# Conv taps, gates, late weights and branch A's projection put in another order in a gated conformer decoder step

## Chip, cores and metric

The kernel runs on one core of a Trainium2 chip. The metric is the device time of one execution in microseconds. The kernel before takes 1085.22 us, the median of 3 runs (1084.03 to 1085.56).

## The reference

One layer of a decoder trunk on 1024 prompt positions plus 16 meta tokens and on 8 x 8 sample positions, all in fp32, with D = 1024 channels:

```python
h = rmsnorm(x, norm_g)
z = jnp.einsum('btd,de->bte', h, w_in)
a_val, a_gate, a_silu, p_in, p_silu, g_a, g_b = jnp.split(z, idx, axis=-1)
u = a_val * jax.nn.sigmoid(a_gate)
c, new_conv = causal_depthwise_conv(u, buf_conv, conv_w, conv_b)   # width 31
c = jax.nn.silu(layernorm(c, ln_g, ln_b)) * jax.nn.silu(a_silu)
br_a = jnp.einsum('btc,cd->btd', c, w_conv_out)
pooled, new_pool = multiscale_pool(p_in, buf_pool, start_pos)      # 4 groups: mean over 2/4/8/16 - token
q = jnp.einsum('btgc,gce->btge', pg, w_pool_mix).reshape(B_, T_, D_POOL)
q = q * pool_scale * jax.nn.silu(p_silu)
br_b = jnp.einsum('btc,cd->btd', q, w_pool_out)
merged = jax.nn.sigmoid(g_a) * br_a + jax.nn.sigmoid(g_b) * br_b
return x + jnp.einsum('btd,de->bte', merged, w_out), new_conv, new_pool
```

A final RMSNorm follows, and the last 30 conv inputs and 15 pool inputs are returned as states.

## The kernel before

Channels lie on the 128 partitions, in 8 blocks of 128; the 1088 positions lie along the free axis, in two halves of 544 (552 with the meta tokens in front). Every fp32 product is made of three products of rounded parts, high x high, high x low and low x high (`gemm`, L149). A *split* makes the parts of an operand: `split` casts the high part on ScalarE and subtracts it on VectorE (L119, L120); `split_dma` casts on ScalarE, negates the high part on ScalarE and lets GpSimd issue a transfer that accumulates the raw operand onto it (L124 to L126).

The stages, with their times in the profiled execution:

1. 0 to 81 us: six of the eight pool input blocks (`pp`) while x and weights arrive, and the RMS norm of x.
2. 88 to 164 us: `Block` products in the order g0 v0 p6 p7 g1 v1 (a conv gate, its value, two pool blocks, and so on), 96 matmuls each (`pg`, `pv`, `pp`).
3. 164 to 683 us: 22 pairs of column blocks in the order g1 v1 g2 v2 g3 v3, q0 to q3 (pool SiLU gate), b0 to b3 (merge gate b), a0 to a3 (merge gate a), s0 to s3 (conv SiLU gate). `seven` makes each pair by a Strassen-type scheme: seven products of 24 matmuls into three PSUM tiles x, v and y. y starts as a copy of x, made by ScalarE (`py`, L467); parts of x are kept in `c2` and `c4`, and VectorE subtracts v from them (L480 for `c4`, which has to read v before the product `d` is added to v, and L489 for `c2`). `put` then evacuates each result with ScalarE (sigmoid or silu, L583). In the q and b pairs the pool mix (`Mix`) puts four products of 12 matmuls (`pmix`) between, whose results a `gate` on VectorE (L832) multiplies with silu of the gate.
4. 683 to 791 us: branch B's projection, `ppo`, 8 output blocks by 2 halves, 48 matmuls each. VectorE multiplies each result with the merge gate `lb` (L997), which SP loads from DRAM.
5. 791 to 830 us: LayerNorm over channels of the conv result: `lcsum` sums the eight blocks, `pt_mean` multiplies it with ones on TensorE, `centre` subtracts the mean (L965), squares on ScalarE (L967) and sums (L969), `suml_var` and `pt_var` give the variance, `root` its inverse root.
6. 830 to 884 us: `branch_a(i)` for each channel block i: times the inverse root (L979), silu on ScalarE (L980), times the gate `lsa` by halves (L982) and a split into the operand `cx`.
7. 882 to 976 us: branch A's projection, `pco`, 8 output blocks d by 2 halves, 48 matmuls each; VectorE multiplies it with `lga` and adds `ltb` (L1068, L1069), and a split gives the operand `mx`. Its first group begins as the `cx` appear.
8. 976 to 1082 us: the product with w_out (`pwo`), the residual and the final norm.

The depthwise conv is VectorE work without a fixed place: per channel block one tap by L661, 30 taps by L663 and four sample groups (L673 to L678). These are pieces in a list, `todo`, with costs. `fill(until)` takes pieces from it while VectorE's modelled time `clock["dve"]` is below `until`; the caller passes TensorE's modelled time, `clock["pe"]`, which `step` advances by 3.0 us for each product. So the written order of VectorE's instructions is set where `fill` is called. Each engine works through its own instructions in the written order (a manual schedule); `defer(n, f)` runs f n steps later. PSUM has four tiles of two banks (`bank2`), weights and halves have pools of fixed size.

## Time and profile before

| | before |
|---|---|
| median of 3 runs | 1085.22 us (1084.03 to 1085.56) |
| the profiled execution | 1084.14 us, its span 1082.4 us |
| TensorE matmul busy | 963.5 us, 89% of the span |
| VectorE busy | 795.6 us, 74% |
| ScalarE busy | 456.1 us, 42% |
| GpSimd busy | 158.7 us, 15% |
| chain that ended last | TensorE 65%, VectorE 14%, ScalarE 9%, DMA 5%, issue 4% |
| granted TensorE clock, mean | 0.94 |

The table is to be read with the stages above: the shares are means over stages in which different engines set the pace. In 500 to 678 us TensorE is busy 175.06 of 178 us; in 818 to 882 us 16.39 of 64 us, at a granted clock of 0.50, which is 1.2 GHz where 1.00 is 2.4 GHz. [...]

### The profile page before, as it was taken

The numbers are of one execution on the slowest core, as the hardware profiler recorded it, in microseconds if no ns is written. First come the engines' busy times: TensorE is split into PE (matmuls) and PEld (weight loads), VectorE is DVE, ScalarE is ACT, GpSimd is POOL, SyncE is SP. The second block draws the span as 40 slices with busy tenths as digits, with TensorE's granted clock in tenths as the row PEclk, the third lists the DMA queues.
The fourth block names the chain that finished last, engine by engine and source line by source line (L and its number), as shares of the span: only waits on it lengthen the run. The fifth ranks groups of instructions, "written<-read, shape, count | busy, mean of one in ns | idle before, by whom it ended". The sixth has DMA issues, their size and how long they took to land.

```text
span 1082.4 us, 17920 instructions
## 1 busy us (share of the span) xinstructions
PE 963.5 (89%) x7032; PEld 932.5 (86%) x7032; DVE 795.6 (74%) x1043; ACT 456.1 (42%) x761; POOL 158.7 (15%) x192
## 2 busy tenths in 40 slices
PE   9997998999999899999999999979921359999996
PEld 8997998999999889999999999979921259998885
DVE  6466869997887698898999998389975554455343
ACT  7634245544554445456555656200035332134111
POOL 0001422322231121232322322000000000000000
PEclk9998999999999899999999999989965559999998
DMA  8333796788695766979889899733430344433222
GB/s 294 114 95 113 215 248 144 162 217 218 146 222 118 202 185 181 256 179 227 190 214 220 200 226 260 262 126 132 167 135 21 83 122 133 132 108 136 98 78 97
DMA packets 100900, 180.67 MB, mean 167 GB/s; under 512 B 21456, under 2 KB 24912, under 8 KB 100816
## 3 DMA queue, kind: packets, MB, share of 16 engines
q1 hardware_dynamic: 70720, 121.98, 35.0%
q0 software_dynamic: 20880, 39.66, 21.2%
q10 hardware_dynamic: 9216, 17.90, 4.4%
q8 instruction: 55, 0.90, 0.3%
q14 instruction: 29, 0.24, 0.1%
HBM read 93.92 MB, written 48.71 MB: 132 GB/s over the span
## 4 chain that ended last, share of the span: by engine, by line
PE 65%; DVE 14%; ACT 9%; DMA 5%; issue 4%; SPq 1%; ACTq 1%; DVEq 0%
PE pco L149 9%; PE ppo L149 7%; PE pp L149 6%; PE px_s L149 5%; PE px_a L149 5%; PE px_q L149 4%; PE pwo L1108 4%; PE px_v L149 3%; PE px_b L149 3%; PE px_g L149 3%; PE pg L149 3%; DVE c L663 2%; PE pv_v L149 2%; DMA xr<-in_xres 2%; PE pv_g L149 1%
## 5 line engine op out<-in xcount | busy, mean ns | idle before, releaser
L663 DVE SCALAR_TENSOR_TENSOR c<-ce,pv,c 128x1024 f32<-128x1024 f32 x240 | 308.1, 1284 | 5.2
L149 PE MATMUL pco<-cx,w_co 128*128 128x272 f32 x768 | 108.4, 303 | 47.5 <-ACT cx L119 47.5
L149 PEld LDWEIGHTS pco<-cx,w_co 128*128 128x128 f32 x768 | 103.9, 200 | 52.1 <-ACT cx L119 50.1
L149 PE MATMUL ppo<-q,w_po 128*128 128x272 f32 x768 | 98.6, 291 | 8.0 <-DVE w_po L120 7.1
L149 PEld LDWEIGHTS ppo<-q,w_po 128*128 128x128 f32 x768 | 97.9, 191 | 8.7 <-DVE w_po L120 7.5
L1108 PE MATMUL pwo<-wo,mx 128*128 128x512 f32 x336 | 79.4, 394 | 0.0
L1108 PEld LDWEIGHTS pwo<-wo,mx 128*128 128x128 f32 x336 | 63.1, 188 | 14.8
L149 PE MATMUL pp<-xg,wh_p 128*128 128x276 f32 x384 | 65.4, 291 | 0.8 <-ACT xg L217 0.5
L149 PEld LDWEIGHTS pp<-xg,wh_p 128*128 128x128 f32 x384 | 54.8, 188 | 1.8 <-ACT xg L217 0.9
L119 ACT CAST mx<-lga 128x544 fp32r<-128x544 f32 x16 | 10.4, 648 | 71.4 <-DVE lga L1069 71.4
L1127 DVE TENSOR_TENSOR xr<-pwo,xr 128x1024 f32<-128x1024 f32 (+1 forms) x9 | 9.9, 1105 | 41.5 <-PE pwo L1108 25.8
L149 PE MATMUL pp<-xg,wl_p 128*128 128x276 f32 x192 | 40.0, 289 | 0.0
L119 ACT CAST w_po<-raw_po 128x512 fp32r<-128x512 f32 x16 | 9.5, 619 | 67.7 <-DMA raw_po<-in_w_po 57.3
L1068 DVE TENSOR_TENSOR lga<-pco,lga 128x544 f32<-128x544 f32 x16 | 11.6, 724 | 33.7 <-PE pco L149 33.7
L1090 ACT ACTIVATE sq<-xr 128x1024 f32<-128x1024 f32 (+1 forms) x9 | 8.7, 965 | 65.5 <-DVE xr L1127 65.5
L149 PE MATMUL px_q<-tT,woq_q 128*128 128x272 f32 x192 | 29.7, 318 | 6.6 <-ACT py_q L467 6.6
L149 PEld LDWEIGHTS px_q<-tT,woq_q 128*128 128x128 f32 x192 | 28.5, 217 | 7.2 <-ACT py_q L467 7.2
L149 PE MATMUL pg<-hx,w_g 128*128 128x276 f32 x192 | 27.3, 306 | 7.0 <-ACT w_g L119 7.0
L149 PEld LDWEIGHTS pg<-hx,w_g 128*128 128x128 f32 x192 | 26.6, 203 | 7.6 <-ACT w_g L119 7.3
L149 PEld LDWEIGHTS pp<-xg,wl_p 128*128 128x128 f32 x192 | 30.2, 188 | 0.0
L149 PE MATMUL px_b<-tT,woq_b 128*128 128x272 f32 x192 | 25.6, 289 | 3.0 <-ACT py_b L467 3.0
L149 PEld LDWEIGHTS px_b<-tT,woq_b 128*128 128x128 f32 x192 | 24.5, 188 | 3.7 <-ACT py_b L467 3.7
(403 smaller groups left out, 2201.3 us busy)
## 6 DMA issues: line engine op xcount, KB each, us to landing
lraw<-d_raw SPq DMA_DIRECT2D x16, 276.0 KB, 3.4
d_pool<-pool SPq DMA_DIRECT2D x8, 544.0 KB, 4.5
lp<-d_pool SPq DMA_DIRECT2D x16, 272.0 KB, 4.8
lq<-d_q SPq DMA_DIRECT2D x16, 272.0 KB, 5.3
lb<-d_sgb SPq DMA_DIRECT2D x16, 272.0 KB, 4.5
d_tb<-lb SPq DMA_DIRECT2D x16, 272.0 KB, 2.1
lsa<-d_sa SPq DMA_DIRECT2D x16, 272.0 KB, 5.2
ltb<-d_tb SPq DMA_DIRECT2D x16, 272.0 KB, 2.8
```

Source lines behind the costliest of these rows:

```text
L119: act.copy(dst_h, src)
L149: pe.matmul(out[:, u, : hi - lo], w(k, a), xs(k, b)[:, lo:hi], start=first and k == ks[0] and i == 0, stop=last and k == ks[-1] and i == 2 ...
L663: dve.scalar_tensor_tensor(c, s, wk, c, ALU.mult, ALU.add)
L1068: dve.tensor_tensor(of_half(ga), ps, of_half(ga), ALU.mult)
L1090: act.activation(sq[:rows, c], xr[:, c], AF.Square, accum_out=a1 if ns[0] else a0)
L1108: pe.matmul(ps[:, n - ns[0]], x(k), wo[k][n][w], start=(k == 0 and s == 0), stop=(k == NK - 1 and s == len(passes) - 1),)
L1127: dve.tensor_tensor(v3(xr[:, c], 512), ps[:, : len(ns)], v3(xr[:, c], 512), ALU.add)
```

## The change

- `LAG`: `fill` goes on until VectorE's modelled time is 1.5 us past the time it is given. In `seven`, in `Mix.gate`, in the glu and in the `ppo` loop `fill` is now called ahead of the evacuation instead of behind it.
- In `seven`, one more `yield` lets the caller issue the copy `py` of a pair one part earlier.
- The first tap of each conv block is made by ScalarE (`begin`), at the first sample group of the block before it.
- The weights of g0 are loaded and split ahead of the norm's products; those of v0 are loaded there.
- In the `ppo` loop the weights of `ppo` 1 to 7 and `w_co0`, `w_co1` are split by `split_dma`, `lb` is loaded one block ahead, and the loads of the conv blocks are spread over two blocks.
- In `branch_a`, `cx` of blocks 1, 3 and 5 is split by `split_dma`.
- The first two output blocks of `pco` are accumulated in four PSUM tiles together, channel block by channel block; `w_co2` is split only afterwards.

```diff
-T_PRODUCT = 3.0
+
+T_PRODUCT, LAG = 3.0, 1.5
...
     plain1(1)
+    ops[0].load()
+    ops[0].split(split)
+    ops[1].load()
     keep_raw(1, 1, outs[1])
     plain1(2)
...
     def fill(until=None):
-        while todo and (until is None or clock["dve"] < until):
+        while todo and (until is None or clock["dve"] < until + LAG):
             if not todo[0]:
                 todo.popleft()
                 continue
             cost, run = todo[0].popleft()
             clock["dve"] += cost
             run()
...
         yield
         y = bank2(f"py_{name}")
         act.copy(y[:, :, :n], x[:, :, :n])
+        yield
         fill(clock["pe"])
         product_of(x, "q2", "T2", False, False)
         c2 = keep("c2")
         fill(clock["pe"])
         product_of(y, "b", "21", False, True)
+        fill(clock["pe"])
         put(0, 0, y[:, :, :n])
-        fill(clock["pe"])
         product_of(x, "q1", "T1", False, False)
         c4 = keep("c4")
         fill(clock["pe"])
@@ -480,12 +489,13 @@
         dve.scalar_tensor_tensor(c4, v[:, :, :n], -1.0, c4, ALU.mult, ALU.subtract)
         spend(2 * n)
         product_of(x, "q4", "22", False, True)
+        fill(clock["pe"])
         put(0, 1, x[:, :, :n])
         yield
-        fill(clock["pe"])
         product_of(v, "d", "T4", False, True)
         put(1, 1, c4)
         yield
+        fill(clock["pe"] - T_PRODUCT)
         dve.scalar_tensor_tensor(c2, v[:, :, :n], -1.0, c2, ALU.mult, ALU.subtract)
         spend(2 * n)
         put(1, 0, c2)
...
@@ -594,7 +604,7 @@
         def put(b, h, z):
             glu(2 * i + b, h, glu_gate.pop((2 * i + b, h)), z)
             if (b, h) in ((0, 1), (1, 0)):
-                Conv(2 * i + b)
+                defer(1, lambda: Conv(2 * i + b))
...
         def __init__(self, i):
             self.i = i
-            work = [(t_op(SEQ) if k else 0.75, lambda k=k: self.taps(k)) for k in range(CW)]
+            work = [(t_op(SEQ), lambda k=k: self.taps(k)) for k in range(1, CW)]
             work.insert(20, (0.0, self.join))
-            work.insert(0, (0.0, self.sample_load))
+            work.insert(0, (0.0, self.begin))
             work += [(1.5, lambda b=b: self.sample(b)) for b in range(0, DB, 2)]
             push(work + [(0.0, self.store)])
...
+
+
+        def begin(self):
+            i = self.i
+            if hasattr(self, "c") or not hasattr(self, "e"):
+                return
+            self.c = slot(f"c{i}", (2, H2))
+            s = v3(self.e[:, META : TP], HP)
+            act.activation(self.c[:, :, :HP], s, AF.Identity, bias=col(OFF_CB, i), scale=col(OFF_CW, i * CW))
...
             wk = col(OFF_CW, i * CW + k)
             s = v3(self.e[:, META + k : TP + k], HP)
-            if k == 0:
-                self.c = slot(f"c{i}", (2, H2))
             c = self.c[:, :, :HP]
-            if k == 0:
-                dve.tensor_scalar(c, s, wk, col(OFF_CB, i), ALU.mult, ALU.add)
-            else:
-                dve.scalar_tensor_tensor(c, s, wk, c, ALU.mult, ALU.add)
+            dve.scalar_tensor_tensor(c, s, wk, c, ALU.mult, ALU.add)
+            if k == 1:
+                self.sample_load()
...
         def sample(self, b):
             i = self.i
+            if b == 0 and self is not chunks[-1]:
+                chunks[chunks.index(self) + 1].begin()
...
         def gate(self, j, h, ps):
             z = pool_gate.pop((j, h))
+            fill(clock["pe"])
             dve.scalar_tensor_tensor(of_half(z), ps, col(OFF_PS, j), of_half(z), ALU.mult, ALU.mult)
             spend(H2)
             defer(1, lambda: sp.dma_start(out=d_q[j][:, h], in_=z))
...
         for h in (0, 1) if left > 1 else (1, 0):
             ps = bank2(f"p{kind}{i}{h}")
             gemm(ps, ops[n], lambda k, s: hx[h][k][:, s], UNITS1, every, True, True)
+            step(2 * T_PRODUCT)
+            if kind == "v":
+                fill(clock["pe"])
             put_block(kind, i, h, ps[:, :, : HT // 2])
-            step(2 * T_PRODUCT)
...
         if kind == "v":
-            Conv(i)
+            defer(1, lambda i=i: Conv(i))
...
     cur = pairs[0][1]
-    next(cur), next(cur)
+    next(cur), next(cur), next(cur)
...
         next(nxt, None)
         if tail:
             mix.gate(*tail)
+        next(nxt, None)
         mix = coming
         after, cur = cur, nxt
...
         for h in range(2):
             dve.tensor_tensor(conv[i][:, h], conv[i][:, h], lsa[i][h], ALU.mult)
-            cx[i].append(operand(f"cx{i}{h}", conv[i][:, h], split))
...
+    lb = {}
+
+    def load_lb(d):
+        if d < NK:
+            lb[d] = [fetch_half(d_sgb[d], h, f"lb{d}") for h in range(2)]
+
+    load_lb(0)
     for d in range(NK):
         (po + co)[d + 2].load()
-        lb = [fetch_half(d_sgb[d], h, f"lb{d}") for h in range(2)]
-        (po + co)[d + 1].split(split)
-        spend(512, 2)
+        load_lb(d + 1)
+        (po + co)[d + 1].split(split_dma)
         for h in range(2):
             ps = gemm_half(f"ppo{d}", po[d], q, h, NK)
-            dve.tensor_tensor(of_half(lb[h]), ps, of_half(lb[h]), ALU.mult)
+            step(2 * T_PRODUCT)
+            if d < 2:
+                load_conv(d * 4 + h * 2, d * 4 + h * 2 + 2)
+            if d == 2 and h == 0:
+                load_sum()
+            if d == 7 and h == 0:
+                co[1].split(split_dma)
+            if d > 0:
+                fill(clock["pe"])
+            z = lb[d][h]
+            dve.tensor_tensor(of_half(z), ps, of_half(z), ALU.mult)
             spend(H2)
-            defer(1, lambda d=d, h=h, z=lb[h]: sp.dma_start(out=d_tb[d][:, h], in_=z))
-            step(2 * T_PRODUCT)
-            if d == 0:
-                load_conv(h * 4, h * 4 + 4)
-                if h:
-                    load_sum()
-            else:
-                fill(clock["pe"])
+            defer(1, lambda d=d, h=h, z=z: sp.dma_start(out=d_tb[d][:, h], in_=z))
     while todo or due:
         fill()
...
@@ -1055,15 +1080,23 @@
             load_merge(d + 1)
         if d + 2 < NK:
             co[d + 2].load()
-        if d + 1 < NK:
+        if 0 < d < NK - 1:
             co[d + 1].split(split)
...
         mx.append([])
+        if d == 0:
+            early = {(d, h): bank2(f"pco{d}{h}") for d in range(2) for h in range(2)}
+            for k in range(NK):
+                for (d_, h), ps in early.items():
+                    gemm(ps, co[d_], lambda k, s: cx[k][h][:, s], UNITS3, (k,), k == 0, k == NK - 1)
         for h in range(2):
-            ps = gemm_half(f"pco{d}", co[d], cx, h, NK)
+            if d < 2:
+                ps = early[d, h][:, :, : H2 // 2]
+            else:
+                ps = gemm_half(f"pco{d}", co[d], cx, h, NK)
             ga = lga[d][h]
             dve.tensor_tensor(of_half(ga), ps, of_half(ga), ALU.mult)
             dve.tensor_tensor(ga, ga, ltb[d][h], ALU.add)
```

How the order of the instructions moves, at three places.

ScalarE, in the q pairs of stage 3, where the products of q1 end and those of q2 begin (`woq1_q2`, `woa_q3`: weight parts; `px20`, `m1`: the pool mix's operands; `c2_q1`, `c4_q1`: evacuations of q1's kept parts; `py_q2`: the copy with which q2's y begins). Before:

```order
L125 ACTIVATE woq1_q2_4116<-woq1_q2_4116 128x512
L583 ACTIVATE c4_q1_3976<-c4_q1_3976 128x544
L124 CAST woa_q3_4166<-a_q3_3942 128x512
L125 ACTIVATE woa_q3_4166<-woa_q3_4166 128x512
L119 CAST px20_4196<-lp20_4097 128x544
L119 CAST px30_4199<-lp30_4099 128x544
L119 CAST m1_4202<-mraw1_4101 128x512
L583 ACTIVATE c2_q1_3899<-c2_q1_3899 128x544
L467 COPY py_q2_4213<-px_q2_3996 128x2x272
```

and now:

```order
L126 ACTIVATE woq1_q2_4122<-woq1_q2_4122 128x512
L593 ACTIVATE c4_q1_3987<-c4_q1_3987 128x544
L125 CAST woa_q3_4170<-a_q3_3953 128x512
L126 ACTIVATE woa_q3_4170<-woa_q3_4170 128x512
L475 COPY py_q2_4204<-px_q2_4011 128x2x272
L120 CAST px20_4206<-lp20_4114 128x544
L120 CAST px30_4209<-lp30_4116 128x544
L120 CAST m1_4212<-mraw1_4118 128x512
```

`py_q2` now stands ahead of the casts of the pool mix and of `c2_q1`, where it stood behind them.

VectorE, at the end of stage 4 and the start of stage 5 (`w0_co0`, `w1_co0`: low parts of weights; `lb50` to `lb71`: the `ppo` products with the merge gate; `c6`, `c7`: conv results; `lc0`: the first block to be centred). Before:

```order
L120 TENSOR_TENSOR w0_co0_8865<-raw0_co0_8722,w0_co0_8865 128x512
L120 TENSOR_TENSOR w1_co0_8868<-raw1_co0_8723,w1_co0_8868 128x512
L997 TENSOR_TENSOR lb70_8861<-ppo70_8871,lb70_8861 128x544
L997 TENSOR_TENSOR lb71_8863<-ppo71_8922,lb71_8863 128x544
L951 TENSOR_TENSOR lcsum_8076<-lcsum_8076,c6_7291 128x1088
L951 TENSOR_TENSOR lcsum_8076<-lcsum_8076,c7_8223 128x1088
L120 TENSOR_TENSOR suml_mean_8976<-lcsum_8076,sumh_mean_8975 128x1088
L965 TENSOR_TENSOR lc0_8013<-lc0_8013,total_mean_8979 128x1088
```

and now:

```order
L1029 TENSOR_TENSOR lb50_8502<-ppo50_8649,lb50_8502 128x544
L1029 TENSOR_TENSOR lb51_8504<-ppo51_8705,lb51_8504 128x544
L967 TENSOR_TENSOR lcsum_8305<-lcsum_8305,c6_7102 128x1088
L967 TENSOR_TENSOR lcsum_8305<-lcsum_8305,c7_8155 128x1088
L121 TENSOR_TENSOR suml_mean_8825<-lcsum_8305,sumh_mean_8824 128x1088
L1029 TENSOR_TENSOR lb60_8637<-ppo60_8772,lb60_8637 128x544
L981 TENSOR_TENSOR lc0_8022<-lc0_8022,total_mean_8878 128x1088
L981 TENSOR_TENSOR lc1_8024<-lc1_8024,total_mean_8878 128x1088
L981 TENSOR_TENSOR lc2_8077<-lc2_8077,total_mean_8878 128x1088
```

`lcsum` and `suml_mean` now stand behind `lb51`, ahead of `lb60`, and the low parts of `w_co0` are no longer made here; on TensorE the products `pt_mean` now stand between `ppo61` and `ppo70`, where they stood behind `ppo71`.

ScalarE, at the end of stage 6 and the start of stage 7 (`cx70`, `cx71`: the last operands of `pco`; `mx00`, `mx01`: the first results; `w0_co1`, `w0_co2`: high parts of the weights of the second and the third output block). Before:

```order
L119 CAST cx60_9144<-c6_7291 128x544
L119 CAST cx61_9148<-c6_7291 128x544
L980 ACTIVATE c7_8223<-c7_8223,pv_74 128x1088
L119 CAST cx70_9154<-c7_8223 128x544
L119 CAST cx71_9158<-c7_8223 128x544
L119 CAST w0_co1_9181<-raw0_co1_8857 128x512
L119 CAST w1_co1_9184<-raw1_co1_8858 128x512
L119 CAST mx00_9238<-lga00_9165 128x544
```

and now:

```order
L996 ACTIVATE c6_7102<-c6_7102,pv_74 128x1088
L120 CAST cx60_9174<-c6_7102 128x544
L120 CAST cx61_9178<-c6_7102 128x544
L996 ACTIVATE c7_8155<-c7_8155,pv_74 128x1088
L120 CAST cx70_9184<-c7_8155 128x544
L120 CAST cx71_9188<-c7_8155 128x544
L120 CAST mx00_9409<-lga00_9195 128x544
L120 CAST mx01_9414<-lga01_9197 128x544
L120 CAST w0_co2_9429<-raw0_co2_9207 128x512
```

The casts of `w_co1` no longer stand here, and those of `w_co2`, which stood behind `mx01` then too, come next after `mx00` and `mx01` as the weights of the first group that TensorE hasn't begun.

## Rows read from the trace of the kernel before

**Rows 1.** TensorE's waits over the whole span: engine, line, releaser, us in total, times, longest.

```profile
PE pco L149 <- ACT cx L119: 47.5, 8, 14.2
...
PE ppo L149 <- DVE w_po L120: 7.1, 2, 6.7
...
PE px_q L149 <- ACT py_q L467: 6.6, 3, 2.9
...
PE px_b L149 <- ACT py_b L467: 3.0, 3, 2.2
```

**Rows 2.** The chain that ended last: start us, us, what held it.

```profile
368.87 3.00 PE px_q L149 x24
...
816.76 1.30 DVE suml_var L120
...
872.24 1.30 ACT c L980
...
879.03 1.30 ACT c L980
881.81 94.15 PE pco L149 x726
```

**Rows 3.** Timeline of TensorE, 80 to 182 us: start, us, instructions, idle before.

```profile
87.80 14.92 PE L149 MATMUL pg<-hx,w_g 128*128 128x276 f32 x96 [7.03 <-ACT w_g L119]
...
139.12 12.35 PE L149 MATMUL pg<-hx,w_g 128*128 128x276 f32 x96
...
174.88 4.76 PE L149 MATMUL px_g<-tT,woq_g 128*128 128x276 f32 x24 [4.87 <-ACT py_g L467]
```

**Rows 4.** Timeline of VectorE, 140 to 176 us.

```profile
157.65 0.73 DVE L700 TENSOR_TENSOR zg<-pv,zg 128x552 f32<-128x552 f32 x1 [7.07 <-issue]
```

**Rows 5.** Timeline of ScalarE, 336 to 372 us.

```profile
358.73 0.66 ACT L583 ACTIVATE c_q<-c_q 128x544 f32<-128x544 f32 x1 [3.22 <-DVE c_q L489]
359.29 0.61 ACT L467 COPY py_q<-px_q 128x544 f32<-128x544 f32 x1
```

**Rows 6.** Timeline of TensorE, 324 to 370 us.

```profile
328.03 4.80 PE L149 MATMUL px_q<-tT,woq_q 128*128 128x272 f32 x24 [1.97 <-ACT py_q L467]
...
349.29 3.27 PE L149 MATMUL pv_q<-tT,wod_q 128*128 128x272 f32 x24
...
359.95 5.81 PE L149 MATMUL px_q<-tT,woq_q 128*128 128x272 f32 x24 [2.85 <-ACT py_q L467]
```

**Rows 7.** Timeline of VectorE, 336 to 364 us.

```profile
344.91 0.78 DVE L832 SCALAR_TENSOR_TENSOR c_q<-pmix,pv,c_q 128x544 f32<-128x544 f32 x1 [3.73 <-PE pmix L149]
...
348.52 0.72 DVE L480 SCALAR_TENSOR_TENSOR c_q<-pv_q,c_q 128x544 f32<-128x544 f32 x1
```

**Rows 8.** Timeline of VectorE, 683 to 800 us.

```profile
708.19 0.72 DVE L997 TENSOR_TENSOR lb<-ppo,lb 128x544 f32<-128x544 f32 x1 [10.21 <-DMA lb<-d_sgb]
...
783.79 1.29 DVE L120 TENSOR_TENSOR w_co<-raw_co,w_co 128x512 fp32r<-128x512 f32 x2
...
789.47 2.60 DVE L951 TENSOR_TENSOR lcsum<-lcsum,c 128x1088 f32<-128x1088 f32 x2
```

**Rows 9.** GpSimd by stretch: us, busy (instructions), TensorE's clock, DMA share, GB/s.

```profile
683.00:791.00 108.00, 0.95 (x3) 0.97 0.45 157
500.00:678.00 178.00, 51.32 (x59) 1.00 0.89 220
```

**Rows 10.** DMA issues by group: KB each, median us from issue to landing.

```profile
woq_a<-q_a POOLq DMA_DIRECT2D x12, 256.0 KB, 4.8
```

**Rows 11.** Timeline of ScalarE, 785 to 900 us.

```profile
893.38 0.65 ACT L119 CAST mx<-lga 128x544 fp32r<-128x544 f32 x1 [5.51 <-DVE lga L1069]
893.93 1.14 ACT L119 CAST w_co<-raw_co 128x512 fp32r<-128x512 f32 x2
```

**Rows 12.** The taps, L663, in 500 to 678 and in 727 to 787 us: ns min/median/max.

```profile
L663 DVE SCALAR_TENSOR_TENSOR c<-ce,pv,c x82: 1272/1284/1405, 505.0 to 675.3; 128x1024 f32<-128x1024 f32 x82
...
L663 DVE SCALAR_TENSOR_TENSOR c<-ce,pv,c x30: 1272/1285/1287, 728.7 to 776.3; 128x1024 f32<-128x1024 f32 x30
```

More of the change, by code (lines that the diff above doesn't have):

```diff
@@ L335, in split_x, with __init__, load, split @@
             hx[h].append(t)
+    class Block:
+        def __init__(self, src, name):
+            self.name, self.src = name, src
+        def load(self):
+            self.raw = [half_raw(f"raw{b}_{self.name}") for b in range(2)]
+            for b in range(2):
+                sp.dma_start(out=self.raw[b], in_=self.src[:, b * NQ : (b + 1) * NQ])
+        def split(self, how=split_dma):
+            self.op = []
+            for b in range(2):
+                o = op_tile(f"w{b}_{self.name}", (2, NQ, P))
+                how(o[:, 0], o[:, 1], self.raw[b])
+                self.op.append(o)
+        def __call__(self, k, s):
+            return self.op[k // NQ][:, s, k % NQ]
+    base = {"p": PG, "g": GG, "v": VG}
+    blocks = [(b[0], int(b[1])) for b in BLOCKS.split()]
+    ops = [Block(w_in[base[kind] + i], f"{kind}{i}") for kind, i in blocks]
     def norm_x(ks):
@@ L375, in fill @@
             run()
-    class Block:
-        def __init__(self, src, name):
-            self.name, self.src = name, src
-        def load(self):
-            self.raw = [half_raw(f"raw{b}_{self.name}") for b in range(2)]
-            for b in range(2):
-                sp.dma_start(out=self.raw[b], in_=self.src[:, b * NQ : (b + 1) * NQ])
-        def split(self, how=split_dma):
-            self.op = []
-            for b in range(2):
-                o = op_tile(f"w{b}_{self.name}", (2, NQ, P))
-                how(o[:, 0], o[:, 1], self.raw[b])
-                self.op.append(o)
-        def __call__(self, k, s):
-            return self.op[k // NQ][:, s, k % NQ]
     class Weights:
@@ L724, in put_block @@
             glu(i, h, sg.pop(h), ps)
-    base = {"p": PG, "g": GG, "v": VG}
-    blocks = [(b[0], int(b[1])) for b in BLOCKS.split()]
-    ops = [Block(w_in[base[kind] + i], f"{kind}{i}") for kind, i in blocks]
-    ops[0].load()
-    ops[1].load()
-    ops[0].split(split)
     t_ops = {"11": hx[0][:NQ], "21": hx[0][NQ:], "22": hx[1][NQ:]}
@@ L982, in branch_a @@
             dve.tensor_tensor(conv[i][:, h], conv[i][:, h], lsa[i][h], ALU.mult)
-            cx[i].append(operand(f"cx{i}{h}", conv[i][:, h], split))
+            cx[i].append(operand(f"cx{i}{h}", conv[i][:, h], split_dma if i in (1, 3, 5) else split))
     finish_a = [(5.0, root)] + [(5.2, lambda i=i: branch_a(i)) for i in range(NK)]
```

## The prediction, on record before the run

> **What bounds the kernel now.** I read the waits of TensorE first, then the chain of waits, then the timelines around each place where TensorE stood. TensorE is the engine that the end follows for most of the span, so each microsecond that it stands idle or runs at half clock on the chain is a microsecond of the run. Its waits [rows 1] show two kinds. The long ones lie late: 47.5 us in eight waits of the projection `pco` for operands that ScalarE casts, 7.1 us before `ppo`. The short ones lie in the Strassen-type products: `px_q` and `px_b` wait 6.6 and 3.0 us for the copy `py`. The chain [rows 2] has the same shape: TensorE products such as the one at 368.87; late, VectorE and ScalarE alone up to `suml_var` at 816.76; then a step of 6.79 us per channel block (872.24 to 879.03, from one silu to the next); then 94.15 us of `pco` from 881.81. The reader is to see a late stretch of some 90 us in which TensorE mostly waits, and ahead of it a long stretch that it nearly fills.
>
> The sum is made against the profiled execution, 1084.14 us for a span of 1082.4; the median of the runs, 1085.22, stands 1.08 above it. A change of under 0.2%, about 2 us, can't be told from none.
>
> **A. The first gate weights earlier.** TensorE stands 7.03 us at 87.80 for the cast of `w_g0`, and the 96 matmuls behind it take 14.92 us where the next gate block's 96 take 12.35: 2.6 us of half clock [rows 3]. The weights now load ahead of the constant transfers and are cast ahead of other work, so up to 9.6 us go there. But the gate product `zg` on VectorE at 157.65 [rows 4] starts the path to the second product of g1, where TensorE waits again, 4.87 us at 174.88 [rows 3]. That path is 17.2 us long and isn't shortened. In the new order the first block's taps stand ahead of `zg`, and by the durations of what stands before it, it starts at about 151.5: 6.2 us earlier. The second wait grows by the rest, and a longer wait may cost another 1 to 1.7 us at half clock (the product behind it took 4.76, one later 3.00 [rows 2, 3]). I take 5; from 3 to 8.
>
> **B. The 22 pairs of products.** In a q pair the copy `py` stands on ScalarE behind `c2`, which waits 3.22 us for VectorE [rows 5]; TensorE waits 2.85 us for `py`, and then `px_q` at 359.95 takes 5.81 [rows 6] against 3.00 for as many matmuls at 368.87 [rows 2]. VectorE is late because it stood 3.73 us at a gate of the pool mix [rows 7] while taps that could have filled the time stood behind the gate in its order. Both causes are removed: `py` is issued ahead of the casts and of `c2`, and `fill` puts taps ahead of each gate. So the 6.6 and 3.0 us [rows 1] go, and with them the half clock behind the two longest, 2.8 and 1.8 [rows 6]: 14.2 in all. The price lies in `c4`. It starts at 348.52 and takes 0.72, and TensorE's `pv_q`, which may not start before it has ended, starts at 349.29 [rows 6, 7]: 0.05 us to spare. Six of the eight q and b pairs have 0.05 to 0.43, the other pairs mostly 1 to 3. `LAG` lets VectorE's list run 1.5 us further ahead of `c4`, so the six pairs lose 0 to 1.5 each; at the middle, 0.7, that is 4.2. I take 10 gained. With no lateness, and the small waits of the other pairs gone too, it is 17; with all six late by 1.5, and waits of that size at the gates' banks as well, 0.
>
> The first taps: eight VectorE operations of 0.8 us go, and eight of about 1.1 (its 1088-wide operations) come onto ScalarE, which has room for them. I cost that at nothing; one that stands ahead of a copy for TensorE costs 1 us once per block, inside the range above.
>
> **C. `ppo` and the mean.** 48 matmuls, one group, take (94.15 - 2.9) / 726 x 48 = 6.03 us in `pco`, where the first 6 us or so run at half clock [rows 2]. From 683.12 on, `ppo` needs 16 such groups, 96.5 us; it took 107.8, with the wait of 6.7 [rows 1] and the half clock behind it. VectorE is the reason: it stood 10.21 us for `lb`, which SP could load only late, and it makes sixteen low parts of weights in this stage, two in 1.29, so 10.4 us [rows 8]. Both go: `lb` is loaded one step ahead, and the low parts become a negation on ScalarE and an accumulating transfer. VectorE's taps and samples ended at 783.79, 100.7 us after 683.12. They lose these 20.6 and some 4.6 of waits for TensorE, and end near +75.5; `lcsum`, which began at 789.47 (+106.4) [rows 8], ends at +78.3, and `suml_mean` at +80.8. In the new order `pt_mean` stands ahead of the last two groups on TensorE, which reaches it at 14 x 6.03 = +84.4; the mean is there at about +87.2. The chain from the mean to `suml_var` took 19.5 us (797.22 to 816.76). Into it come three `lb` products of 0.7, and a hold of some 1.7 by the eight casts and negations of `w_co` on ScalarE. That puts `suml_var` at +110.5 where it was at +133.6 [rows 2]: 23 us. The last two groups of `ppo` hide under the centring. GpSimd, which issues the new transfers, is idle here: 0.95 us busy in 683 to 791 [rows 9]. Bounds: 17 if late low parts keep TensorE 6 us in all, 26 if ScalarE's hold and the `lb` products find gaps.
>
> **D. Branch A.** Each 6.79 us step [rows 2] holds two low parts on VectorE, 0.72 each, and 0.71 of waiting for each one's cast. In blocks 1, 3 and 5 they become negations and transfers, the two products follow each other, and the next silu can start after about 4.7. Three steps of 2.1 are 6.2; I take 6, from 3 (ScalarE's four operations in the way) to 7. The low part lands some 5 us after its issue [rows 10], which TensorE can bear, since it has more room than work here.
>
> **E. `pco` by channel.** Before, TensorE did 6 matmuls per channel block and waited; 6 + 15 x 48 were left at 881.81, done in 94.15 us [rows 2]. Now four banks take 24 per block, at half clock 24 x 0.25 = 6.0 us, which about fits a step, and behind the last block's cast 24 + 12 x 48 are left. Twelve groups are 72.4 us. They can't start at once: the casts of `w_co2` now stand on ScalarE behind `mx00` and `mx01` (such a cast takes 0.65, the two of a weight 1.14 [rows 11]). From the end of the cast `cx70`: VectorE's own last operations 2.8, two evictions of 2 x 0.72, a cast 0.65, the weight's casts 1.14, its low part 0.65, hand-overs 0.4, about 8.5. So 8.5 + 72.4 and 2 for a restart below full clock are 83 against 94.15: 11. If the groups waited for nothing, it would be 6.0 + 72.4, a gain of 15.7; with the casts 2 us later and 2.8 of half clock [rows 6] at two restarts, 7.
>
> Sum: 5 + 10 + 23 + 6 + 11 = 55; 1084.14 - 55 = 1029.1, and 1.08 more against the median: **1030**. What follows `pco`, the projection with `w_out`, keeps its order and its length.
>
> **The rivals.**
> *Only the tail gains.* The early wait moves on to `px_g`, and the q and b pairs trade `py` for `c4`; A and B come to nothing and 40 stay: 1045. For it: the 0.05 us of room [rows 6, 7], and a path behind `zg` that isn't shorter. Against: 14 us of waits have a cause that the order removes.
> *No wait for `w_co2`, no price in `c4`.* B gives 17 and E 15.7: 1018. Against: the order puts those casts last.
> *Low parts late in `ppo`.* A raw weight lands, is cast and negated (1.2), and the transfer lands 4.8 after its issue [rows 10]. If each of seven steps holds TensorE 2 us, and the product behind runs at half clock as in [rows 6], 2.8 more, 34 us come back: 1064. Against: each step is 12 us long and GpSimd is idle.
> *Slower than before: VectorE behind everywhere.* `LAG`, 1.5, and a tap of 1.28 that has begun make 2.8 us. If VectorE runs so far behind in all 22 pairs and has no room left, each pair holds TensorE 2.8 us at `d`: 61.6 us lost against 45 won in A, C, D and E, so 1102. It decides from 45 / 22 = 2.0 us a pair. For it: VectorE's list lasts to the end of this stretch, so `fill` always finds a tap. Against: most pairs had 1 to 3 us to spare, and VectorE loses 6.5 us of first taps and its standing at gates.
> *Taps slowed by transfers.* A tap's median is 1284 ns in 500 to 678, beside 51.32 us of GpSimd work, and 1285 in 727 to 787, with almost none [rows 9, 12]: no slowing. The Trainium skill (GPSIMD Engine Reference, 1. Specifications) lists GpSimd's SBUF interfaces as shared with VectorE, with contention for VectorE instructions with two inputs from SBUF, which the taps are. The medians here disagree; single taps reach 1405. If each of 20 new transfers in `ppo` held a tap for the 0.87 us that an issue lasts (51.32 / 59 [rows 9]), 17 us of C were lost: 1047.
>
> **How the numbers follow.** Forecast 0.55; only the tail 0.20; no wait for `w_co2` 0.11; low parts late 0.05; slower 0.04; slowed taps 0.03; 0.02 that the new order leaves the waits as they are. The forecast's own range is 1021 to 1040. The low ends (3 + 0 + 17 + 3 + 7 = 30) give 1055 and the high ends (8 + 17 + 26 + 7 + 15.7 = 74) 1011; the range, 1012 to 1054, holds the forecast, the tail case, the case at 1018 and the slowed taps, less some of their wings. Faster 0.94, same 0.02, slower 0.04.
>
> **What would show it.** Right: no wait of `pg` for `w_g0`, `px_g` still waiting; no wait of `px` for `py` in q and b; `pt_mean` ahead of `ppo7`; `suml_var` about 110 us behind the first `ppo`; silus 6.8 and 4.7 us apart by turns; one wait of `pco` for `w_co2` of about 4 us, and about 83 us from `cx70` to the end of `pco`. Wrong: waits of `pv` for `c4` of over 1 us in many pairs, waits of `ppo` for a transfer, silus that stay 6.8 apart, a wait for `w_co2` over 6 us.

## The result, and the profile after

The changed kernel takes 1029.81 us, the median of 4 runs (1027.86 to 1031.34); the kernel before, run beside it, 1084.81 (1084.03 to 1085.56). The ratio is 0.9492, with a 95% interval of 0.9473 to 0.9511. The profiled execution of the changed kernel took 1030.44 us for a span of 1028.7, so its span is set against 1082.4.

The head of its page: the span and the busy times (963.5 us of TensorE and 795.6 of VectorE before).

```profile
span 1028.7 us, 17986 instructions
...
PE 956.8 (93%) x7032; PEld 930.3 (90%) x7032; DVE 774.1 (75%) x1011; ACT 478.6 (47%) x793; POOL 177.1 (17%) x216
```

Its waits of TensorE, in the columns of [rows 1].

```profile
PE pco L150 <- ACT cx L120: 14.2, 1, 14.2
PE pt_var L194 <- ACT sumh_var L120: 11.6, 1, 11.6
PE pco L150 <- DMA cx<-lc: 10.7, 6, 3.9
PE px_q L150 <- ACT py_q L475: 4.5, 2, 2.5
PE px_g L150 <- ACT py_g L475: 4.4, 1, 4.4
PE px_s L150 <- ACT c_s L465: 3.6, 2, 2.0
PE pco L150 <- ACT w_co L120: 3.3, 1, 3.3
PE px_b L150 <- ACT py_b L475: 2.3, 2, 1.8
```

The long waits shrank: `pco` waited 47.5 us for the casts of `cx` [rows 1], now 14.2 (the first one alone), though 10.7 for the transfers of `cx` and 3.3 for `w_co` have come in; and `ppo` no longer stands among them. The short ones did not go: `px_q` for `py` 4.5 where it was 6.6, `px_b` 2.3 where it was 3.0, and `px_s` has a wait for `c_s`, 3.6, that is new in its size. The chain says the same of the later stages.

```profile
671.43 84.05 PE ppo L150 x668
...
780.07 1.30 DVE suml_var L121
...
812.90 1.30 ACT lc L996
817.56 1.19 ACT lc L996
...
829.30 4.79 DMA cx<-lc
834.14 8.01 PE pco L150 x46
848.58 73.37 PE pco L150 x572
921.95 44.46 PE pwo L1141 x192
```

One stretch `ppo` of 84 us without a break, `suml_var` at 780.07 where it was at 816.76 [rows 2], silus some 4.6 us apart where a block is split by transfers, and `pco` from 848.58 on without a break.

Cut at the same events in both traces, the 53.7 us divide as follows. The first column names the part of the prediction that speaks of the stretch.

| part | stretch, by its ends | before | after | gained | forecast |
|---|---|---|---|---|---|
| A | start to the product `d` of g1 | 191.73 | 185.82 | 5.9 | 5 |
| B | to the first `ppo` | 491.39 | 484.50 | 6.9 | 10 |
| C | to the first `pt_var` | 133.66 | 109.77 | 23.9 | 23 |
| D | to the end of the cast `cx70` | 64.97 | 58.22 | 6.7 | 6 |
| E | to the end of `pco` | 94.21 | 83.64 | 10.6 | 11 |
| | to the end of the span | 106.44 | 106.75 | -0.3 | 0 |

Such a stretch is not the same in every execution. In the profiled executions of the runs below that leave a stretch as it is, A takes 185.5 to 187.7 us, B 484.2 to 484.9, C 109.7 to 109.8, D 58.2 and E 83.1 to 84.1. Most of what A varies lies ahead of the first gate product `pg`, which starts between 80.4 and 82.5 us in the changed kernel and the eleven runs below that are built on it.

Four parts came within 1 us of the forecast, B 3 us short. So the experiments ask two things: whether each part's gain has the cause that was named, and why B is smaller. The place behind q1 that the prediction read before [rows 5 to 7] answers the second for the most part: q1 is one of the four pairs that hold a mix, q1, q2, q3 and b0. ScalarE, VectorE and TensorE there, after the change, in one timeline each:

```profile
349.76 0.60 ACT L475 COPY py_q<-px_q 128x544 f32<-128x544 f32 x1 [5.04 <-DVE c_q L845]
```

```profile
342.47 6.56 DVE L677 SCALAR_TENSOR_TENSOR c<-ce,pv,c 128x1024 f32<-128x1024 f32 x5
348.95 0.78 DVE L845 SCALAR_TENSOR_TENSOR c_q<-pmix,pv,c_q 128x544 f32<-128x544 f32 x1
```

```profile
344.75 3.16 PE L150 MATMUL pv_q<-tT,woq_q 128*128 128x272 f32 x24
350.42 4.81 PE L150 MATMUL px_q<-tT,woq_q 128*128 128x272 f32 x24 [2.51 <-ACT py_q L475]
```

`py_q` no longer stands behind `c2`, but it waits 5.04 us all the same, and for something else: the gate `c_q` on VectorE (L845), which reads the last of the mix's four products. That gate starts at 348.95 behind five taps (6.56 us from 342.47), and the copy begins as it ends. The copy reads nothing that the gate makes. What ties them is the PSUM tile: there are four, x and v of q2 and the v of q1 that `c2` has still to read hold three, and the one that comes free for y is that of the product which the gate reads. The change took the copy out of one queue and put the gate that frees its tile at the end of another.

### The profile page after: what moved, and what is told of

It is laid out like the page before. It is cut to its first block, busy times and chain, and to the rows that moved or that the text cites. A ratio compares the mean times of both kernels' runs of the same rounds, so it can differ in the third digit from the quotient of the medians.

```text
span 1028.7 us, 17986 instructions
## 1 busy us (share of the span) xinstructions
PE 956.8 (93%) x7032; PEld 930.3 (90%) x7032; DVE 774.1 (75%) x1011; ACT 478.6 (47%) x793; POOL 177.1 (17%) x216
## 4 chain that ended last, share of the span: by engine, by line
PE 74%; DVE 11%; ACT 6%; DMA 5%; issue 3%; SPq 1%; DVEq 0%; ACTq 0%; POOLq 0%; POOL 0%
PE pp L150 9%; PE ppo L150 8%; PE pco L150 8%; PE px_b L150 5%; PE px_a L150 5%; PE pwo L1141 4%; PE px_s L150 4%; PE px_q L150 4%; PE px_v L150 4%; PE px_g L150 3%; DVE c L677 3%; PE pg L150 2%; PE pv_a L150 2%; PE pv_v L150 2%; DMA xr<-in_xres 2%
## 5 line engine op out<-in xcount | busy, mean ns | idle before, releaser
L150 PE MATMUL pco<-cx,w_co 128*128 128x272 f32 x768 | 110.2, 308 | 28.3 <-ACT cx L120 14.2
L150 PEld LDWEIGHTS pco<-cx,w_co 128*128 128x128 f32 x768 | 106.9, 206 | 31.7 <-ACT cx L120 14.9
L150 PE MATMUL pmix<-px,m 128*128 128x272 f32 x192 | 27.1, 289 | 0.5 <-DVE zq L845 0.5
L150 PE MATMUL px_s<-tT,woq_s 128*128 128x272 f32 x192 | 25.4, 288 | 2.0 <-ACT c_s L465 2.0
```

What stands on the lines that cost most here:

```text
L150: pe.matmul(out[:, u, : hi - lo], w(k, a), xs(k, b)[:, lo:hi], start=first and k == ks[0] and i == 0, stop=last and k == ks[-1] and i == 2 ...
```

## The experiments

All times are medians of 4 runs, each taken beside the kernel before, which took 1084.56 to 1084.88 us there. The first eight and e10 differ from the changed kernel in the lines shown; where a stretch is named, it is one of the table above.

### e1: the gates without the fill

```diff
         def gate(self, j, h, ps):
             z = pool_gate.pop((j, h))
-            fill(clock["pe"])
             dve.scalar_tensor_tensor(of_half(z), ps, ...
```

> The changed kernel with the fill ahead of the pool mix's gates taken out. Theory (the copy py needs the PSUM tile that the fourth product of the mix holds, and that is freed by a gate behind five taps on VectorE): without the taps ahead of the gate py comes in time, the waits of px_q and px_b for py (6.8 us in all) fall below 1.5 and the half clock behind two of them goes; 6 to 10 us faster than the changed kernel, about 1021. Rival (VectorE is simply behind in the q and b pairs, wherever its taps stand): the waits stay at 5 or more, or move to pv for c4, and the time stays within 2 us of 1030.

1023.98 us (1023.10 to 1025.64), ratio to before 0.9442 [0.9417, 0.9468]: 5.8 faster than the changed kernel by the medians, 7.4 by the spans (1021.3 for 1028.7). Its waits of TensorE hold no line of `px_q` or `px_b` any more; `c4` has come in their place, with less.

```profile
PE pv_q L150 <- DVE c_q L489: 1.6, 2, 0.8
...
PE pv_b L150 <- DVE c_b L489: 1.3, 2, 0.8
```

```profile
345.78 0.60 ACT L475 COPY py_q<-px_q 128x544 f32<-128x544 f32 x1 [1.04 <-DVE c_q L844]
```

The copy still follows the gate (L844 here), but at 345.78, 1.04 us after ScalarE was ready for it. Part B becomes 478.1 us, a gain of 13.3. That settles the late gate as the cause of the waits, and the trace has the copy released by it both times though it reads nothing of the gate's, which leaves the tile as the tie; the rival, a VectorE that is late wherever its taps stand, would have kept them.

### e2: no lag

```diff
-T_PRODUCT, LAG = 3.0, 1.5
+T_PRODUCT, LAG = 3.0, 0.0
```

> The changed kernel with LAG 0 for 1.5. Theory (the gate's place behind taps makes the waits): the fourth gate stands behind five taps in this order too, so the waits for py stay within 1.5 us of 6.8 and the time within 2 us of 1030. Rival (the lag of 1.5 us makes VectorE late): each of the four waits falls by 1.5, to under 1.5 us in all, and the time falls by 5 to 8.

1028.38 us (1027.46 to 1030.56), ratio 0.9484 [0.9458, 0.9510], which can't be told from the changed kernel. The waits are the same four.

```profile
PE px_q L150 <- ACT py_q L475: 4.5, 2, 2.5
...
PE px_b L150 <- ACT py_b L475: 2.2, 2, 1.8
```

So `LAG`, on which the forecast's price for `c4` rested, does nothing for these waits, and nothing that shows in the time. Around the gate VectorE's order has the five taps without it too:

```profile
342.11 6.56 DVE L677 SCALAR_TENSOR_TENSOR c<-ce,pv,c 128x1024 f32<-128x1024 f32 x5
348.59 0.78 DVE L845 SCALAR_TENSOR_TENSOR c_q<-pmix,pv,c_q 128x544 f32<-128x544 f32 x1
```

### e3: the copy py late again

```diff
         act.copy(y[:, :, :n], x[:, :, :n])
-        yield
...
-    next(cur), next(cur), next(cur)
+    next(cur), next(cur)
...
             mix.gate(*tail)
-        next(nxt, None)
```

> The changed kernel with the copy py issued where it was before (the extra yields undone), the rest kept. Theory (the earlier copy gives 0.45 us in each of the pairs without a mix): those pairs take 21.48 us each again where they take 21.03, so 465 to 650 us grows by 3.5 to 4, and the q and b pairs lose 0 to 5 more; 1034 to 1039. Rival (that gain comes from the fills that moved behind, not from py): the pairs stay at 21.0 and the time within 2 us of 1030.

1062.60 us (1061.55 to 1065.05), ratio 0.9804 [0.9773, 0.9836]: 32.8 slower than the changed kernel, far beyond both expectations. Seven waits of 3.1 to 5.1 us for `py` stand in this run: at the end of q0 and of each of the four pairs with a mix, and one each before a value and an s pair. Behind six of them the 24 matmuls take 4.6 to 5.8 us, with half clock in them, where they take 3.3 without:

```profile
PE px_q L150 <- ACT py_q L475: 13.0, 3, 5.0
...
PE px_b L150 <- ACT py_b L475: 8.5, 4, 3.6
PE px_s L150 <- ACT py_s L475: 5.6, 4, 5.1
...
PE px_v L150 <- ACT py_v L475: 3.5, 1, 3.5
```

Here B takes 516.4 us, 25 more than in the kernel before, which issues `py` at the same place. What differs in this stretch is the place of the fills, and the first taps on ScalarE, which I didn't try apart (`LAG` does nothing, e2): with them `py` waits behind a `c2` that is later still. VectorE makes that of q1 7.4 us after the end of the product `d`, where it was 5.4 us before. My reading of the pairs without a mix held in kind: from the product `d` of b1 to that of s2 they take 194.4 us here, 189.3 in the changed kernel and 193.0 before.

### e4: zg ahead of the taps

```diff
-            if kind == "v":
+            if kind == "v" and left > 1:
                 fill(clock["pe"])
             put_block(kind, i, h, ps[:, :, : HT // 2])
```

> The changed kernel without the fill ahead of the last value block's evacuation, so that zg does not stand behind six taps on VectorE. Theory (the first gate weights gained only 6 of 9.6 us since the path from zg to px_g bounds): zg starts up to 3.7 us earlier, at about 147.6, px_g's wait falls from 4.4 to 0.5 to 2 us, and the half clock behind it goes too: 4 to 6 us faster, about 1025. Rival (another operand of that path is late, a weight or T part that waits for a transfer): the wait stays over 3 us and the time within 2 us of 1030.

1026.99 us (1025.60 to 1028.24), ratio 0.9468 [0.9442, 0.9494]: 2.8 faster by the medians. By the traces A gains 2.1 us more (185.82 to 183.71), though stage 1, which the edit doesn't touch, ended 1.4 us later in this execution; from the start of `pg` to the product `d` of g1 it is 101.77 us for 105.28, 3.5 less. In this run:

```profile
81.94 12.37 PE L150 MATMUL pg<-hx,w_g 128*128 128x276 f32 x96
```

```profile
149.19 0.73 DVE L718 TENSOR_TENSOR zg<-pv,zg 128x552 f32<-128x552 f32 x1 [3.02 <-PE pv L150]
```

```profile
166.43 5.25 PE L150 MATMUL px_g<-tT,woq_g 128*128 128x276 f32 x24 [4.88 <-ACT py_g L475]
```

`zg` starts 67.25 us behind the start of `pg` where it is 70.75 in the changed kernel, so 3.5 of the 3.7 us are there, and now it waits 3.02 us for TensorE's own product. The theory had the wrong wait go: that of `px_g` stays, 4.88, as the path from `zg` to `px_g` is as long as ever (17.2 us in both kernels and here), and the three short waits of `pv_g` ahead of it, 2.9 us in the changed kernel, are gone. e11 and e12, which hold this edit too, take 101.4 and 101.9 us from `pg` to `d`, the runs without it that keep `LAG` 104.7 to 105.5.

### e5: w_co2 early

```diff
-        if 0 < d < NK - 1:
+        if 1 < d < NK - 1:
             co[d + 1].split(split)
...
                     gemm(ps, co[d_], lambda k, s: cx[k][h][:, s], UNITS3, (k,), k == 0, k == NK - 1)
+            co[2].split(split)
```

> The changed kernel with w_co2 split ahead of the evacuations of the first two output blocks. Theory (the third block waits 3.35 us only for the casts of w_co2, which stand behind mx00 and mx01 on ScalarE): that wait goes, 847.7 becomes about 844.4, and the end comes 3 to 5 us earlier, about 1026. Rival (the PSUM tile of pco00 comes free too late, since VectorE now makes two low parts ahead of lga00): a wait of 2 us or more of pco for lga, and the time within 2 us of 1030.

1026.29 us (1024.87 to 1027.18), ratio 0.9458 [0.9444, 0.9472]: 3.5 faster than the changed kernel; from `cx70` to the end of `pco` 78.5 us for 83.6. The changed kernel's wait, and the same place here:

```profile
834.14 10.25 PE L150 MATMUL pco<-cx,w_co 128*128 128x272 f32 x64 [0.31 <-DMA cx<-lc]
847.74 12.52 PE L150 MATMUL pco<-cx,w_co 128*128 128x272 f32 x83 [3.35 <-ACT w_co L120]
```

```profile
832.42 1.40 PE L150 MATMUL pco<-cx,w_co 128*128 128x272 f32 x6 [2.68 <-DMA cx<-lc]
835.20 35.08 PE L150 MATMUL pco<-cx,w_co 128*128 128x272 f32 x262 [1.37 <-DMA cx<-lc]
```

The wait for `w_co` is gone and nothing takes its place: 262 matmuls run on from 835.20.

### e6: pco by halves

```diff
-        if d == 0:
-            early = {(d, h): bank2(f"pco{d}{h}") for d in range(2) for h in range(2)}
...
-            if d < 2:
-                ps = early[d, h][:, :, : H2 // 2]
-            else:
-                ps = gemm_half(f"pco{d}", co[d], cx, h, NK)
+            ps = gemm_half(f"pco{d}", co[d], cx, h, NK)
```

> The changed kernel with the first two output blocks of pco accumulated half by half as before, the rest kept. Theory (by channel, 18 of 24 matmuls per block are done in branch A's gaps, less the wait for w_co2): from the cast of cx70 to the end of pco 94 us again where it is 83.6, so 9 to 12 slower than the changed kernel, about 1040. Rival (branch A's steps or the clock set the gain, not the order of the matmuls): under 5 slower.

1039.98 us (1038.90 to 1040.76), ratio 0.9585 [0.9571, 0.9599]: 10.2 slower than the changed kernel, of which 9.2 lie between `cx70` and the end of `pco` (92.8 us). The by-channel order is the cause of most of E's 10.6.

### e7: all cx on VectorE

```diff
-            cx[i].append(operand(f"cx{i}{h}", conv[i][:, h], split_dma if i in (1, 3, 5) else split))
+            cx[i].append(operand(f"cx{i}{h}", conv[i][:, h], split))
```

> The changed kernel with cx of blocks 1, 3 and 5 split on VectorE as before. Theory (each transfer takes two low parts and the wait for their casts out of a step): silus 6.8 us apart throughout, the last cx70 6.4 later, the time 4.5 to 6.5 slower, about 1035. Rival (the low parts that land late, 10.7 us of TensorE's waits, are on the path and eat the gain): within 2 us of 1030.

1037.00 us (1035.60 to 1038.86), ratio 0.9559 [0.9541, 0.9577]: 7.2 slower; by the traces 5.3, of which D is 6.8 longer and E 1.1 shorter. The silus stand 6.80 us apart again. So the waits for late transfers, 10.7 us in the changed kernel, are off the path but for about 1 us; and that the 1.1 is theirs isn't shown, since the wait for `w_co` is 1.6 us here for 3.3.

### e8: the late weights' low parts on VectorE

```diff
-        (po + co)[d + 1].split(split_dma)
+        (po + co)[d + 1].split(split)
+        spend(512, 2)
...
-                co[1].split(split_dma)
+                co[1].split(split)
+                spend(512, 2)
```

> The changed kernel with the late weights' low parts (w_po1 to 7, w_co0, w_co1) on VectorE, lb still loaded one block ahead. Theory (VectorE's list ended the stage: 10.4 us of low parts and 10.2 of standing for lb): the conv work ends some 10 us later, lcsum too, TensorE waits for pt_mean or for a weight behind taps, and suml_var comes 4 to 10 us later: 1034 to 1040. Rival (only the late lb held VectorE, and the conv work has room): within 2 us of 1030. Other rival (the whole of the 24 us is the low parts): 15 or more slower.

1039.42 us (1036.72 to 1041.55), ratio 0.9578 [0.9554, 0.9602]: 9.6 slower. C takes 118.45 us, 8.7 more than in the changed kernel. VectorE, and TensorE:

```profile
759.14 2.61 DVE L967 TENSOR_TENSOR lcsum<-lcsum,c 128x1088 f32<-128x1088 f32 x2
```

```profile
672.01 96.08 PE L150 MATMUL ppo<-q,w_po 128*128 128x272 f32 x764 [0.34 <-DVE w_po L121]
767.93 0.29 PE L194 MATMUL pt_mean<-sumh_mean,ones 128*128 128x272 f32 x1
```

`lcsum` starts 15 us later than in the changed kernel (744.18), `pt_mean` stands behind the whole of `ppo`, and nothing of the centring is hidden. `ppo` itself runs without a break, so the low parts cost the mean, and not TensorE's weights. Not all of it is VectorE's time: the conv work ends 6.6 us later than in the changed kernel, counted from the first `ppo`, and between its end and `lcsum` the order now has three evacuations of `ppo` and six low parts, where it had two evacuations. Of C's 23.9 us the transfers, with the order that they allow, are 8.7; the other 15 stay without them.

### e9: only the early copy, on the kernel before

```diff
         act.copy(y[:, :, :n], x[:, :, :n])
+        yield
...
-    next(cur), next(cur)
+    next(cur), next(cur), next(cur)
...
             mix.gate(*tail)
+        next(nxt, None)
```

> The kernel before with one thing of the change: the copy py issued earlier (the extra yields), all fills where they were. Theory (the early copy is what gains in the 22 pairs, and the fills ahead of the gates give part of it back): the 22 pairs and the last one gain at least as much as the 7 us of the whole change, 7 to 14 in all, so 1071 to 1078. Rival (copy and fills only work together): under 4 us gained or slower, 1081 or more.

1070.47 us (1070.10 to 1071.98), ratio 0.9868 [0.9853, 0.9882]: 14.4 faster than before, with three places changed. B takes 477.2 us, 14.2 less than before, twice the gain of the whole change there. The waits for `py` are gone from its list of q and b pairs, and `c4` waits little:

```profile
PE px_s L149 <- ACT c_s L457: 2.7, 2, 1.5
...
PE pv_b L149 <- DVE c_b L481: 1.1, 1, 1.1
...
PE pv_q L149 <- DVE c_q L481: 0.8, 1, 0.8
```

With e1 and e3 this divides B: the early copy gives 14.2, the rest of the change takes 7.3 of it back, and the fill ahead of the gates accounts for 6.4 of those (e1). This holds for the copy put first; the parts don't simply add, as taking the copy back out of the changed kernel costs B 31.9 (e3). Of the 14.2, 11.5 lie between the products `d` of q0 and of b1, and 3.5 in the pairs from there to s2.

### e10: lb late again

```diff
-    load_lb(0)
     for d in range(NK):
         (po + co)[d + 2].load()
-        load_lb(d + 1)
+        load_lb(d)
```

> The changed kernel with lb loaded in its own block's step as before, the low parts still made by transfers. Theory (lb and the low parts share the 24 us of this stage; the low parts alone gave 9): VectorE stands for lb again, suml_var comes 4 to 12 us later, 1034 to 1042. Rival (the stand of 10 us for lb came from the eight conv loads that stood ahead of it on SP, which the change spreads over two blocks): no stand over 2 us, within 2 us of 1030.

1032.01 us (1030.12 to 1032.95), ratio 0.9508 [0.9492, 0.9524]. C takes 109.76 us, the same as with the early load; the 2 us lie ahead of the product `d` of g1, which this edit doesn't touch. VectorE at the second block's `lb`, which stood 10.21 us for its load [rows 8]:

```profile
702.20 0.71 DVE L1028 TENSOR_TENSOR lb<-ppo,lb 128x544 f32<-128x544 f32 x1
```

It starts as the taps ahead of it end, without a stand. SP issues that load at 685.16 here and at 700.13 before, where two stores of results, six loads of conv blocks and that of `lcsum` stood ahead of it in this stage. So the early load was not needed. What took the stand away isn't shown: the load is issued 15 us earlier by the loads' spreading and the place of the stores, and VectorE comes to it only behind taps, which the change wrote ahead of this evacuation. I didn't try these apart.

### e11 and e12: four edits together

e11 puts e1, e4 and e5 together and adds one edit: `pt_mean` is issued as soon as its operands stand in the order, and not a step later.

```diff
-        defer(1, run)
+        run() if name == "mean" else defer(1, run)
```

> Four edits on the changed kernel: no fill ahead of the mix's gates, none ahead of the last value block's evacuation, w_co2 split ahead of the first evacuations, and pt_mean issued at once, so between the two halves of ppo6 and not behind them. Theory (the waits are independent, and the mean is ready to be multiplied 6 us before TensorE reaches it): 5.8 + 2.8 + 4.5 from the single runs and 5 to 6 for the mean, 1010 to 1013. Rival (the mean's chain meets a VectorE that still has products of ppo to evacuate): the mean gives under 2 us, 1015 to 1018.

1009.60 us (1009.21 to 1012.55), ratio to before 0.9310 [0.9292, 0.9328]: 20.2 faster than the changed kernel, 0.4 us below the range that the single runs and the mean added up to (1010 to 1013). C takes 104.38 us, 5.4 less:

```profile
740.01 0.29 PE L194 MATMUL pt_mean<-sumh_mean,ones 128*128 128x272 f32 x1
...
741.01 18.21 PE L150 MATMUL ppo<-q,w_po 128*128 128x272 f32 x144
765.41 0.59 PE L194 MATMUL pt_var<-sumh_var,ones 128*128 128x272 f32 x1 [6.19 <-ACT sumh_var L120]
```

`pt_mean` runs ahead of `ppo61`, and three halves of `ppo` are hidden under the centring, not two.

e12 is e11 with `cx` of block 5 split on VectorE (`i in (1, 3)`).

> The kernel of the four edits with cx of block 5 split on VectorE again, 1 and 3 by transfers. Theory (with the weight of the third block ready, TensorE's late low part of block 5 is on the path, 4 us of waits, against 2.1 us that the transfer saves in the steps): within 2 us of the run with all three. Rival (the steps alone set the end): 2 us slower. Other rival (the waits do): 2 to 3 faster.

1013.05 us (1010.93 to 1014.19), ratio 0.9334 [0.9313, 0.9354]: by the traces 3.8 us longer between `pt_var` and the end of `pco` (139.4 for 135.6). Of these 2.2 lie in D, as the transfer's saving in the steps had it; the other 1.5 lie in E and are not much more than E varies. The steps set the end, and the late low part of block 5 isn't worth avoiding.

## Why the prediction was right, and where it wasn't

**The total** came out at 1029.8 for 1030 since four of five terms were sized well and the fifth was 3 us too large, with the small errors of the others in sum to the other side. That it came within 0.2 us is luck: the fifth term was two wrong ones that partly cancel, and stretch A alone varies by 2 us between executions.

**A** held by its own steps, 5.9 here and 4.0 to 6.2 by the other runs, for 5. `pg` starts at 80.54 without a wait, `zg` at 151.29 where I had about 151.5, and the wait moved to `px_g`, as was said:

```profile
80.54 12.38 PE L150 MATMUL pg<-hx,w_g 128*128 128x276 f32 x96
...
168.51 5.30 PE L150 MATMUL px_g<-tT,woq_g 128*128 128x276 f32 x24 [4.36 <-ACT py_g L475]
```

```profile
151.29 0.73 DVE L718 TENSOR_TENSOR zg<-pv,zg 128x552 f32<-128x552 f32 x1
```

The prediction had that wait grow by the rest of 9.6 us; it stayed at 4.36, as TensorE was held by operands of `pv_g` ahead of it, 2.9 us in three short waits. Both kinds hang on `zg`, which the taps written ahead of it hold up by 3.5 us (e4).

**B** is where a step failed: "Both causes are removed: `py` is issued ahead of the casts and of `c2`, and `fill` puts taps ahead of each gate." The first half was right and gave 14.2 us (e9), just the sum of waits and half clock that I had put there. That it is the same to the tenth is chance: the sum set two durations of a timeline, 5.81 and 4.80 [rows 6], against 3.00 of the chain, where the timeline has 3.27, so its rows give 13.7; and the gain came in part from other pairs: 11.5 us came from those with a mix and 3.5 from the later ones, which I had left to the upper end of the range. The second half was wrong in sign. VectorE's standing idle at the gates was not the loss; the taps that fill the time delay the gate, and the gate frees the tile of `py` (e1). The price that I did charge, 4.2 us for `c4` by `LAG`, was not paid at all: TensorE never waited for `c4` in the changed kernel, and without the lag the time is the same (e2). So a wrong price of 4.2 stood for a give-back of 7.3, of which 6.4 are the fill ahead of the gates (e1) and 0.8 lie at the end of the stretch. The 0.05 us for `c4` that the rows showed was hardly room: at 383.16 in the kernel before, TensorE waited 0.78 us for `c4`, and there too the product starts 0.05 us behind its end. As soon as the gates go first, that place is paid for: 0.6 to 0.8 us in four pairs of e1. A small loss that no step named lies at the end of the stretch: from the product `d` of s2 to the first `ppo` 26.2 us for 24.4 (25.4 with the copy alone, e9), with the waits of `px_s` for `c_s`; ScalarE makes that copy at 657.64, after 2.29 us in which the trace names a store (`d_sa`) as what it waits for. I tried nothing on it, so its cause stays open.

**C** held as a sum, 23.9 for 23, and in its order: conv ends, `lcsum` starts at 744.18 (+73.9, where I had +75.7), `pt_mean` at +85.0, `suml_var` at +109.75 where I had +110.5. Its division was partly off. The low parts on VectorE were worth 8.7 (e8), for the 10.4 of VectorE time that I counted, but the lead of `lb`, to which I gave the stand of 10.21 us, was worth nothing once the rest was in place (e10). One thing I did not see: `suml_mean` was ready at 749.25 and TensorE came to `pt_mean` at 755.32, 6 us later; e11 takes 5.4 of them.

**D** and **E** held: 6.7 for 6 and 10.6 for 11, undone by e7 and e6 at 6.8 and 9.2. The silus stand 6.8 and 4.6 us apart by turns, for 6.8 and 4.7. The third block began 9.4 us behind `cx70`, with 8.5 forecast, and its wait of 3.35 had the named cause (e5). The late low parts that I had called bearable cost about 1 us, if that (e7).

**The rivals.** *Only the tail gains* is refuted by A and B, 12.8 us together. *No wait for `w_co2`, no price in `c4`* was half true, in the half that concerns `c4`. *Low parts late in `ppo`*: `ppo` waited for nothing after its first matmuls. *VectorE behind everywhere* is refuted as a whole, but its kind is real: the late gates of four pairs were a VectorE behind, and with the copy late (e3) B took 25 us more than in the kernel before, which I took to be such lateness without trying it apart. *Taps slowed by transfers* is refuted in the stage itself, where GpSimd now issues:

```profile
L677 DVE SCALAR_TENSOR_TENSOR c<-ce,pv,c x33: 1273/1285/1354, 683.9 to 735.4; 128x1024 f32<-128x1024 f32 x33
```

```profile
671.00:757.00 86.00, 15.14 (x17) 1.00 0.81 234
```

A tap's median is 1285 ns beside 15.14 us of GpSimd work, as it was beside 0.95 us [rows 9, 12]. The single long ones don't go with the transfers. Of the changed kernel's 240 taps, 102 run beside GpSimd's issuing of a transfer and no other work of GpSimd, and none of them takes over 1290 ns; the four that take over 1300 ns, 1473 at most, are all among the 16 that run beside a copy which GpSimd makes itself.

## What to carry to other kernels

Before work is put into an engine's idle time ahead of an instruction, ask who waits for that instruction: here five taps ahead of a gate held a PSUM tile, which held a copy, which held TensorE, and with the taps behind the gate those waits were gone, for 0.6 to 0.8 us at `c4` in four pairs. When a copy, a cast or an evacuation is late, look for every queue and every buffer that it needs, since moving it out of one only shows the next. A sum over stages that comes out right can hold two wrong terms of opposite sign; single edits undone on the chip, cut at the same events of the trace, are what tells them apart.

## What the runs showed of the hardware that I had not expected

Waits of about the same length had different sequels in TensorE's granted clock. In the changed kernel a wait of 1.96 us before `px_q` was followed by 24 matmuls in 4.76 us, at a mean granted clock of 0.65, so in good part at 1.2 GHz; waits of 1.77 and 2.03 us were followed by 24 in 3.28 and 3.25 at a granted clock of 1.00, which is 2.4 GHz. In e3 even one of 3.09 us was followed by 24 in 3.26, at 1.00:

```profile
381.22 4.76 PE L150 MATMUL px_q<-tT,woq_q 128*128 128x272 f32 x24 [1.96 <-ACT py_q L475]
```

```profile
439.67 3.28 PE L150 MATMUL px_b<-tT,woq_b 128*128 128x272 f32 x24 [1.77 <-ACT py_b L475]
```

```profile
328.22 3.26 PE L150 MATMUL px_q<-tT,woq_q 128*128 128x272 f32 x24 [3.09 <-ACT py_q L475]
```

So the length of a wait of 2 to 3 us did not decide by itself whether half clock followed. In a sum such a wait is worth a range, from nothing to the 1.5 us more that the first took, and not a fixed price.
